# The feed-forward head of a two-layer encoder: the projection's last tiles and the norm's sums in a new order

## The chip, the cores and the metric

The kernel runs on one core of a Trainium2 chip. A core has a matrix engine (PE, with its weight loads shown apart as PEld), a vector engine (VectorE, DVE in the rows), a scalar engine (ScalarE, ACT), a general engine (GpSimd, POOL) and an engine that issues transfers (SyncE, SP). Each has its own queue and works it off in order; they meet at semaphores. The metric is the device time of the whole kernel in microseconds (us).

## The reference, cut to what matters

Two sequences, one of 256 and one of 512 tokens of width 1024, run through two layers and a last norm. Layer 0 mixes with an mLSTM, layer 1 with windowed attention; both then have the same feed-forward part.

```python
for l in range(DEPTH):                       # 2
    mod = silu(c) @ adaln_w[l] + adaln_b[l]  # sh1, sc1, g1, sh2, sc2, g2
    h = rmsnorm(x, norm_g[l, 0]) * (1 + sc1) + sh1
    y = mixer(h)                             # ends with a projection: ... @ w_out
    x = x + g1 * y
    h = rmsnorm(x, norm_g[l, 1]) * (1 + sc2) + sh2
    x = x + g2 * conv_ffn(h, w_up, conv_w, conv_b, w_down)
return rmsnorm(x, final_g)
```

All is float32. The change sits where the mixer's projection ends (`x = x + g1 * y`), the second norm follows (`rmsnorm(x, norm_g[l, 1])`), and the feed-forward's first products begin.

## The kernel before, in words

The 768 tokens stand side by side, columns of tiles with 128 features as rows; they are worked in two halves of 384. A float32 weight is split into a high part in the matmul's format (cast on ScalarE, `whi`, L260) and the low rest (difference on VectorE, `wlo`, L261); a product takes three matmuls: high by high, high by low, low by high.

**The projection** (`out_proj`, L592) is a generator. It makes 16 tiles of 128 features by 384 tokens: tiles 0 to 7 for the first half, 8 to 15 for the second. The weights come from another generator (`tiles`, L596): a tile's weights are loaded, cast and split only when the loop at L619 asks for them. Tiles 8 to 10 use weights that are still there; those of tiles 11 to 15 are loaded again. A tile is 24 matmuls into one of four fixed PSUM banks (tile i goes to bank (i + 2) mod 4), then the residual sum on VectorE (L590), then its square on ScalarE (L111). The generator stops ahead of tile 8 and of tile 15, in each case with that tile's weights already fetched. The weights' high parts and low parts have three buffers each, the raw loads five.

**The norm** (`Norm`, L90). The first six of a half's eight squares are summed on VectorE (L115) as they come; the other two stay apart. So the mean over features is taken on PE from three tiles: three tiles by three blocks of 128 tokens, each a matmul against a column of 1/1024; every one of them is two instructions in the trace, 18 in all. ScalarE adds epsilon (L150), GpSimd raises to the power -1/2 (L153), PE broadcasts the result over the rows (6 instructions), and `apply` (L1095) scales, shifts and, for the second half, forms the combinations of quarters that the feed-forward's products need (T1 to T4, by a scheme with seven products for eight). The first half's `apply` is issued whole; the second's is a generator whose steps the head calls one by one. Its first work on VectorE is the difference of two shifts, `dsh` (L1108), a tile of 128 x 4.

**The head** (`head`, L1257, called at L1412) begins the feed-forward while the projection ends. It stands in a block with a manual schedule for PE, ScalarE and VectorE (L1411): what the block issues on these three runs in the order in which it is written. Everything else is ordered by a planner that simulates the engines; instructions from outside the block may be put between those of the block. GpSimd and SyncE are the planner's throughout. The head as written before the change:

1. loads of the first two weight units (`ra`, `rb`, twice);
2. two "marks": small matmuls that open banks 2 and 3 (L1276, L1436);
3. split of `ra[0]` (`wa[0]`); the weight sums `sums(0)` (L1279: four differences and sums of 512 columns, one more for the low part of the sum, one cast); split of the result (`wc[0]`);
4. the rest of the projection, that is tile 15 with residual sum and square (L1300);
5. the product B11 by `wa[0]` (12 matmuls), the copy of its bank to `r1` (L1189), the norm's mean, `sums(1)`, the split `wc[1]`, the product B21 into the same bank, the copies to `r1` (L1182), the norm's broadcast and its first combination (L1304 to L1311);
6. the other products, with the norm's steps between (from L1313).

**Behind the head** the pairs of feed-forward units follow (`pair`, L1194). A pair's weight sums run on GpSimd (L1202, L1205, L1206, L1214). For the first pairs, `issue_after` (L1420) queues their instructions on ScalarE and VectorE behind two instructions that the head returns; those on GpSimd are free. So the pair's first sums may run on GpSimd while the head works.

Of the kernel before, what the change touches and what calls it, by code (L numbers as in the profile page):

```python
# [11 lines left out]
F32 = mybir.dt.float32  # L12
# [72 lines left out]
def pieces(c0, c1):  # L85

    return [(max(c0, s0), min(c1, s1), q) for q, (s0, s1) in enumerate(SEQS) if max(c0, s0) < min(c1, s1)]


class Norm:  # L90
# [16 lines left out]
    def square(self, c):  # L107

        net = self.net
        sq = net.tmp([P, self.n])  # L110
        net.nc.scalar.activation(sq, self.x(c), AF.Square)  # L111
        self.sums.append(sq)
        if 2 <= len(self.sums) and self.count < KC - self.on_pe:
            acc = self.sums[0]
            self.adds.tensor_tensor(acc, acc, self.sums.pop(), ALU.add)  # L115
        self.count += 1
# [3 lines left out]
    def begin(self, n):  # L120

        if self.pm is None:
            self.pm = self.net.pa()
            self.sides = [self.pm[:, 2 * b : 2 * b + 2] for b in range(self.n // P)]
            self.done = 0
        for i in range(self.done, n):
            for b, o in enumerate(self.sides):

                self.net.nc.tensor.matmul(
                    o, self.sums[i][:, b * P : (b + 1) * P], self.net.inv,  # L130
                    start=i == b == 0, stop=i == KC - 1, skip_group_check=True,
                )
        self.done = max(self.done, n)

    def stages(self):
# [17 lines left out]
        nc.gpsimd.tensor_tensor(r, r, net.mhalf[:, :nb], ALU.pow)  # L153
# [14 lines left out]
class Net:  # L168
# [423 lines left out]
    def out_proj(self, u0, act, xt, l, apply):  # L592
# [16 lines left out]
        norms = [Norm(self, xt, half, apply, last=True, adds=self.nc.vector) for half in HALVES]  # L609
# [9 lines left out]
        for i, (z, c, w) in enumerate(todo):  # L619
            if i in (KC, 2 * KC - 1):  # L620
                yield
            c0, c1, _ = HALVES[z]
            o = self.ps()[:, : c1 - c0]
            self.product(o, w, act, c0, c1, range(self.begun.pop(i, 0), KC))
            self.tick(4.2)
            for p0, p1, q in pieces(c0, c1):
                self.resid(xt, o[:, p0 - c0 : p1 - c0], l, 16, c, (p0, p1, q))
            norms[z].square(c)
            if i % KC == KC - 1:
                self.start(HALVES[z], norms[z].stages())  # L630
# [443 lines left out]
    def combined(self, l, i, pool):  # L1074
# [19 lines left out]

        def apply(x, pr, rng):  # L1095
            if rng[0] == 0:
                for c in range(KC):
                    full[c] = one(F32)
                    modulate(full[c], c, x, pr, rng)
                    put((self.B11, self.B21)[c // 4], c % 4, full[c])  # L1100
                return
# [5 lines left out]
            dsh = pool.tile([P, 4], F32, name="dsh")  # L1107
            nc.vector.tensor_tensor(  # L1108
                dsh, self.mod[l][:, 24 * i + 4 : 24 * i + 8, q], self.mod[l][:, 24 * i : 24 * i + 4, q], ALU.subtract
            )  # L1110
# [73 lines left out]
    def outset(self, o, w, r1):  # L1184
# [3 lines left out]
        self.quarters(o, part(0), self.B11, True)  # L1188
        self.nc.scalar.copy(r1[:, col(H) :], o)  # L1189
        yield  # L1190
        self.quarters(o, part(1), self.B21, False)
# [65 lines left out]
    def head(self, u0, last_tile, pool, urows, mark, early):  # L1257
# [21 lines left out]
        def sums(i):  # L1279
# [4 lines left out]
            tt(s2, s1_, s2, ALU.subtract)  # L1284
            tt(s4, s4, s2, ALU.subtract)
            tt(s1[i][1], s1_, s1[i][0].bitcast(F32), ALU.subtract)
            tt(s1_, a22, s2, ALU.subtract)

# [9 lines left out]
        sums(0)  # L1298
        wc[0] = self.split(ra[0])
# [4 lines left out]
        first = self.outset(fixed(0), wa[0], rows[0][0])  # L1304
        next(first)
        step()
        sums(1)
        wc[1] = self.split(ra[1])
        next(first, None)

        step()  # L1311
# [57 lines left out]
        return act.ins, dve.ins  # L1369
# [298 lines left out]
```

## Time and profile before

| what | value |
|---|---|
| median of 3 runs | 1844.58 us (1842.21 to 1845.0) |
| profiled execution | 1843.78 us, its span 1842.0 |
| PE busy | 1793.2 us, 97% of the span |
| VectorE busy | 1367.0 us, 74% |
| ScalarE busy | 895.3 us, 49% |
| GpSimd busy | 488.0 us, 26% |
| mean granted clock of PE | 0.994 |
| the head of layer 0 | from about 500 us |
| the head of layer 1 | from about 1290 us |

How to read the rows. In the order of time a row has the start, the duration, the engine, the line of the kernel, the operation, output and input tiles, their shape and the count; in brackets stands how long the engine had been idle and what ended that. Matmuls are pipelined: a row's duration reaches over the start of the next, so that the distance of starts is the cost. In the view by windows a row has the stretch, its length, the busy time of PE, PEld, DVE, ACT and POOL with their counts, the granted clock of PE (1.00 is full speed), the share of the transfer engines and GB/s. The chain of waits is the work that ended last, followed back from the end.

### The profile page before, as it was taken

How to read it: one execution, taken by the hardware profiler on the slowest of the kernel's cores; microseconds unless marked ns; L12 is line 12 of the kernel's file. 1: busy time of each engine (PE TensorE's matmuls, PEld its weight loads, DVE VectorE, ACT ScalarE, POOL GpSimd, SP SyncE). 2: the span in 40 equal slices, each digit the busy share in tenths (PEclk: the TensorE clock that was granted, in tenths of full speed). 3: DMA queues.
4: the chain of work that ended last, by engine and by line, in shares of the span. 5: the costliest groups of instructions: out<-in, count | busy, mean ns of one | idle time of the engine just before them, and what ended most of it. 6: DMA issues, size and time to landing. Idle time of an engine off the chain costs nothing.

```text
span 1842.0 us, 28931 instructions
## 1 busy us (share of the span) xinstructions
PE 1793.2 (97%) x11290; PEld 1657.4 (90%) x11290; DVE 1367.0 (74%) x2101; ACT 895.3 (49%) x1815; POOL 488.0 (26%) x386
## 2 busy tenths in 40 slices
PE   6999999999999999999999999999999999999997
PEld 3987887889998999999999999889989999999997
DVE  4755676886689877777777757766898777777776
ACT  4443443354456444444444556765564444444443
POOL 1001001021024333333331313430144333333322
PEclk9999999999999999999999999999999999999999
DMA  8344566546312221222223321124122222222212
GB/s 330 119 145 134 172 195 221 164 138 219 101 46 74 76 61 66 69 69 69 69 69 93 104 83 50 53 94 129 50 86 69 69 69 69 69 69 70 69 35 69
DMA packets 64245, 184.48 MB, mean 100 GB/s; under 512 B 6167, under 2 KB 23831, under 8 KB 64108
## 3 DMA queue, kind: packets, MB, share of 16 engines
q1 hardware_dynamic: 64108, 182.63, 30.8%
q8 instruction: 89, 1.46, 0.3%
q14 instruction: 48, 0.39, 0.1%
HBM read 176.17 MB, written 6.43 MB: 99 GB/s over the span
## 4 chain that ended last, share of the span: by engine, by line
PE 86%; DVE 6%; DMA 3%; ACT 2%; issue 1%; POOL 1%; SPq 0%; POOLq 0%; ACTq 0%; DVEq 0%
PE ps L254 27%; PE pa L254 25%; PE ps L1169 10%; PE ps L1172 10%; PE ps L1170 10%; PE pa L1008 1%; DMA slab<-in_adaln_w_dram 1%; DMA raw<-in_w_dram 1%; DVE wlo L261 1%; DVE ada L506 1%; DVE slab L590 1%; DMA raw<-in_adaln_w_dram 0%; PE pa L1172 0%; PE pa L1169 0%; PE pa L1170 0%
## 5 line engine op out<-in xcount | busy, mean ns | idle before, releaser
L260 ACT CAST whi<-raw 128x1024 fp32r<-128x1024 f32 x237 | 247.9, 1048 | 350.4 <-PE pa L254 161.4
L261 DVE TENSOR_TENSOR wlo<-raw,whi 128x1024 fp32r<-128x1024 f32 x237 | 316.6, 1337 | 119.8 <-ACT whi L260 117.3
L254 PE MATMUL pa<-slab,whi 128*128 128x256 f32 (+1 forms) x1472 | 346.6, 331 | 3.2 <-DVE slab L590 3.2
L254 PEld LDWEIGHTS pa<-slab,whi 128*128 128x128 f32 x1472 | 252.7, 188 | 27.5 <-DVE slab L590 4.5
L590 DVE SCALAR_TENSOR_TENSOR slab<-pa,mod,slab 128x256 f32<-128x256 f32 (+1 forms) x368 | 211.2, 592 | 70.8 <-PE pa L254 70.5
L254 PE MATMUL pa<-slab,wlo 128*128 128x256 f32 (+1 forms) x736 | 233.9, 330 | 0.0
L254 PE MATMUL ps<-zh,whi 128*128 128x256 f32 (+1 forms) x560 | 189.0, 339 | 2.3 <-ACT whi L260 1.7
L254 PE MATMUL ps<-zh,wlo 128*128 128x256 f32 (+1 forms) x560 | 184.1, 330 | 2.0 <-DVE wlo L261 2.0
L254 PE MATMUL ps<-zl,whi 128*128 128x256 f32 (+1 forms) x560 | 185.1, 332 | 0.0
L1169 PE MATMUL ps<-zh,whi 128*128 128x384 f32 x504 | 172.3, 342 | 3.6 <-ACT nt L1240 1.8
L1170 PE MATMUL ps<-zl,whi 128*128 128x384 f32 x504 | 169.9, 337 | 0.8 <-DVE zl L1126 0.8
L1172 PE MATMUL ps<-zh,wlo 128*128 128x384 f32 x504 | 168.9, 335 | 0.0
L254 PEld LDWEIGHTS pa<-slab,wlo 128*128 128x128 f32 x736 | 138.5, 188 | 13.1 <-DVE wlo L261 0.4
L1205 POOL TENSOR_TENSOR raw<-raw,raw 128x512 f32<-128x512 f32 x40 | 52.2, 1305 | 330.8 <-DVE wlo L261 259.4
L254 PE MATMUL ps<-slab,whi 128*128 128x384 f32 x512 | 132.0, 339 | 0.9 <-DVE slab L261 0.5
L1402 POOL TENSOR_TENSOR slab<-slab 128x772 f32<-128x772 f32 x44 | 86.5, 1967 | 164.6 <-DVE slab L1390 152.7
L1389 DVE SCALAR_TENSOR_TENSOR slab<-slab,cstt,slab 128x771 f32<-128x771 f32 x88 | 103.6, 1179 | 26.6 <-ACT slab L1387 26.5
L254 PEld LDWEIGHTS ps<-zh,whi 128*128 128x128 f32 x560 | 107.4, 192 | 15.9 <-issue 4.4
L506 DVE SCALAR_TENSOR_TENSOR ada<-raw,silc,ada 128x1024 f32<-128x1024 f32 x84 | 110.6, 1354 | 14.9 <-DMA raw<-in_adaln_w_dram 14.8
L1202 POOL TENSOR_TENSOR raw<-raw 128x512 f32<-128x512 f32 x40 | 68.5, 1712 | 200.1 <-DMA raw<-in_w_dram 169.7
L254 PEld LDWEIGHTS ps<-zh,wlo 128*128 128x128 f32 x560 | 107.2, 192 | 12.2 <-DVE wlo L261 2.9
L254 PEld LDWEIGHTS ps<-zl,whi 128*128 128x128 f32 x560 | 107.4, 192 | 11.9 <-issue 3.4
(291 smaller groups left out, 4265.7 us busy)
## 6 DMA issues: line engine op xcount, KB each, us to landing
raw<-in_w_dram SPq DMA_DIRECT2D x208, 512.0 KB, 3.7
raw<-in_adaln_w_dram SPq DMA_DIRECT2D x84, 512.0 KB, 4.6
slab<-in_x_dram SPq DMA_DIRECT2D x12, 512.0 KB, 6.8
slab<-in_adaln_w_dram SPq DMA_DIRECT2D x12, 512.0 KB, 10.3
slab<-mrows SPq DMA_DIRECT2D x8, 384.0 KB, 5.3
xs<-slab SPq DMA_DIRECT2D x6, 512.0 KB, 3.6
bt<-brow SPq DMA_DIRECT2D x16, 192.0 KB, 3.0
slab<-xs SPq DMA_DIRECT2D x6, 512.0 KB, 6.9
```

The source lines that it names most:

```text
L254: self.nc.tensor.matmul(out, lhsT, rhs, start=start, stop=stop)
L260: nc.scalar.copy(hi, src)
L261: return nc.vector.tensor_tensor(lo, src, hi.bitcast(F32), ALU.subtract)
L506: stt(acc[:, s], row, w, acc[:, s], ALU.mult, ALU.add)
L590: self.nc.vector.scalar_tensor_tensor(x, o, self.mod[l][:, gc + c, q : q + 1], x, ALU.mult, ALU.add)
L1169: mm(o, wh[:, k], hi[k], start=start and k == 0, stop=False, skip_group_check=True)
L1170: mm(o, wh[:, k], lo[k], start=False, stop=False, skip_group_check=True)
L1172: mm(o, wl[:, k], hi[k], start=False, stop=k == 3, skip_group_check=True)
L1202: tt(q[2], q[2], q[3], ALU.add)
L1205: tt(q[0], q[2], q[0], ALU.subtract)
L1389: stt(y[:, 1:], u[:, :-1], w(0), y[:, 1:], ALU.mult, ALU.add)
L1402: nc.gpsimd.tensor_tensor(y, y, yrow[:, j], ALU.mult)
```

## The change

Five things.

- The projection's generator stops ahead of tile 14 instead of tile 15, and for tiles 14 and 15 also between product and residual sum and behind the square. The head resumes it step by step, with the weight sums `sums(0)` and `sums(1)`, now generators too, in between. So tile 14 comes into the block, behind the marks, and so does all that the generator issues when it is resumed.
- In this order the first weight sums come ahead of tile 14's residual sum, the second's first two ahead of tile 15's.
- The first half sums all eight squares on VectorE (`on_pe` 0), the second seven (`on_pe` 1): the mean has one and two tiles on PE instead of three. The second half's first tile goes to PE right behind tile 15 (`begin(1)`), the other after eight matmuls of B11.
- `outset` takes the norm's steps into the products: B11's first eight matmuls, the mean, its last four, the copy, B21's first eight, the broadcast, its last four.
- `dsh` is formed in the first half's `apply`. The head also returns the norm's power, so that the first pairs' instructions on GpSimd are queued behind it.

```diff
 class Norm:
     def square(self, c):
         ...
         self.sums.append(sq)
-        if 2 <= len(self.sums) and self.count < KC - self.on_pe:
+        self.count += 1
+        if not self.held:
+            self.add()
+
+    def add(self):
+        if 2 <= len(self.sums) and self.count <= KC - self.on_pe:
             acc = self.sums[0]
             self.adds.tensor_tensor(acc, acc, self.sums.pop(), ALU.add)
-        self.count += 1
+
+    held = False
...
-        for i in range(self.done, n):
+        last = min(KC, self.on_pe + 1) - 1
+        for i in range(self.done, min(n, last + 1)):
...
-        nc.gpsimd.tensor_tensor(r, r, net.mhalf[:, :nb], ALU.pow)
+        self.power = nc.gpsimd.tensor_tensor(r, r, net.mhalf[:, :nb], ALU.pow)

 def out_proj(...)
-        norms = [Norm(self, xt, half, apply, last=True, adds=self.nc.vector) for half in HALVES]
+        norms = [Norm(self, xt, half, apply, i, last=True, adds=self.nc.vector) for i, half in enumerate(HALVES)]
+        self.norm = norms[1]
...
         for i, (z, c, w) in enumerate(todo):
-            if i in (KC, 2 * KC - 1):
+            late = i >= 2 * KC - 2
+            if i in (KC, 2 * KC - 2):
                 yield
             ...
             self.tick(4.2)
+            if late:
+                norms[z].held = True
+                yield
             for p0, p1, q in pieces(c0, c1):
                 self.resid(xt, o[:, p0 - c0 : p1 - c0], l, 16, c, (p0, p1, q))
             norms[z].square(c)
+            if late:
+                yield

 def combined(...)
+        dsh = pool.tile([P, 4], F32, name="dsh")
+
         def apply(x, pr, rng):
             if rng[0] == 0:
+                s = self.mod[l][:, 24 * i : 24 * i + 8, 0]
+                nc.vector.tensor_tensor(dsh, s[:, 4:], s[:, :4], ALU.subtract)
...
-    def outset(self, o, w, r1):
+    def outset(self, o, w, r1, low=None):
-        self.quarters(o, part(0), self.B11, True)
+        self.quarters(o, part(0), self.B11, True, low)
         self.nc.scalar.copy(r1[:, col(H) :], o)
         yield
-        self.quarters(o, part(1), self.B21, False)
+        self.quarters(o, part(1), self.B21, False, low)

 def head(...)
         def sums(i):
             ...
             tt(s2, s1_, s2, ALU.subtract)
+            yield
             tt(s4, s4, s2, ALU.subtract)
+            yield
             tt(s1[i][1], s1_, s1[i][0].bitcast(F32), ALU.subtract)
             tt(s1_, a22, s2, ALU.subtract)
+            yield
...
         wa[0] = self.split(ra[0])
-        sums(0)
-        wc[0] = self.split(ra[0])
+        ops = [sums(i) for i in range(2)]
+        next(ops[0])
+        next(ops[0])
+        wc[0], low = split(ra[0])
+        next(last_tile)
+        next(last_tile)
+        next(ops[0])
+        low()
+        self.norm.add()
+        next(last_tile)
+        self.norm.begin(1)
+        next(ops[1])
+        next(last_tile)
+        next(ops[1])
+        wc[1], low = split(ra[1])
+        next(ops[1])
+        low()
         for _ in last_tile:
             pass
         norm = self.take(HALVES[1])
         step = lambda n=1: [next(norm, None) for _ in range(n)]
-        first = self.outset(fixed(0), wa[0], rows[0][0])
+        first = self.outset(fixed(0), wa[0], rows[0][0], step)
         next(first)
-        step()
-        sums(1)
-        wc[1] = self.split(ra[1])
         next(first, None)
-        step()
...
-        return act.ins, dve.ins
+        return act.ins, dve.ins, self.norm.power.ins
```

More of the change, by code (lines that the diff above doesn't have):

```diff
@@ L130, in begin @@
                     o, self.sums[i][:, b * P : (b + 1) * P], self.net.inv,
-                    start=i == b == 0, stop=i == KC - 1, skip_group_check=True,
+                    start=i == b == 0, stop=i == last, skip_group_check=True,
                 )
@@ L1106, in apply @@
             sh = lambda c: self.mod[l][:, 24 * i + c, q : q + 1]
[L1107 to L1110, printed above, removed]
             def scale(c):
```

## The prediction

> **What bounds the kernel now.** I read the page's busy times and its chain first, then the waits of the matmul engine, then the order of time around the feed-forward head of layer 0 (500 to 520 us) on each engine, then layer 1 for the same places, and last the granted clock wherever PE had been idle. The page, its busy line and its chain:
>
> ```profile
> span 1842.0 us, 28931 instructions
> PE 1793.2 (97%) x11290; PEld 1657.4 (90%) x11290; DVE 1367.0 (74%) x2101; ACT 895.3 (49%) x1815; POOL 488.0 (26%) x386
> PE 86%; DVE 6%; DMA 3%; ACT 2%; issue 1%; POOL 1%; SPq 0%; POOLq 0%; ACTq 0%; DVEq 0%
> ```
>
> PE sets the end, so the change is worth the matmuls it takes out and the gaps it closes or opens on PE in two places, one per layer. A stretch of layer 0, from the view by windows (its length, then PE's busy time): PE has no gap in the six tiles ahead of the head.
>
> ```profile
> 477.60:501.40 23.80, 23.80 (x147) 23.80 (x146) 18.87 (x37) 16.29 (x36) 0.85 (x1) 1.00 0.29 90
> ```
>
> PE alone in order of time (start, duration, x count): marks, tile 15, B11, the 18 small matmuls of the mean, B21, the broadcast of the norm, and the next product.
>
> ```profile
> 505.57 0.52 PE L254 MATMUL ps<-yh 128*128 128x384 f32 x2
> 505.93 0.52 PE L254 MATMUL ps<-slab,whi 128*128 128x384 f32 x2
> ...
> 510.12 0.34 PE L1169 MATMUL ps<-yh,whi 128*128 128x384 f32 x1
> ...
> 512.21 2.06 PE L254 MATMUL pa<-inv,nt 128*128 128x2 f32 x18
> 514.13 0.42 PE L1169 MATMUL ps<-yh,whi 128*128 128x384 f32 x1
> ...
> 516.12 0.34 PE L1172 MATMUL ps<-yh,wlo 128*128 128x384 f32 x1
> 516.93 0.93 PE L254 MATMUL pa<-kct,nr 128*128 128x128 f32 x6 [0.47 <-POOL nr L153]
> ```
>
> A tile's 24 matmuls take 510.12 - 505.93 = 4.19 us, 0.175 each; the 18 of the mean take 514.13 - 512.21 = 1.92, 0.107 each. The broadcast could have gone at 516.30 and went at 516.93.
>
> VectorE, ScalarE and GpSimd there:
>
> ```profile
> 498.20 1.04 ACT L260 CAST whi<-raw 128x1024 fp32r<-128x1024 f32 x1
> 501.56 0.62 DVE L590 SCALAR_TENSOR_TENSOR slab<-ps,mod,slab 128x384 f32<-128x384 f32 x1
> 502.10 0.55 DVE L115 TENSOR_TENSOR nt<-nt,nt 128x384 f32<-128x384 f32 x1
> 505.77 0.62 DVE L590 SCALAR_TENSOR_TENSOR slab<-ps,mod,slab 128x384 f32<-128x384 f32 x1 [0.93 <-PE ps L254]
> 508.06 0.69 DVE L1286 TENSOR_TENSOR s1l<-raw,s1h 128x512 fp32r<-128x512 f32 x1
> 508.78 0.69 DVE L1287 TENSOR_TENSOR raw<-raw,raw 128x512 f32<-128x512 f32 x1
> 509.39 1.22 DVE L261 TENSOR_TENSOR wlo<-raw,whi 128x1024 fp32r<-128x1024 f32 x1
> 511.17 0.53 ACT L111 ACTIVATE nt<-slab 128x384 f32<-128x384 f32 x1 [1.86 <-DVE slab L590]
> 512.40 0.48 ACT L1189 COPY slab<-ps 128x384 f32<-128x384 f32 x1 [0.71 <-PE ps L1172]
> 514.30 1.30 POOL L1205 TENSOR_TENSOR raw<-raw,raw 128x512 f32<-128x512 f32 x1 [5.94 <-DMA raw<-in_w_dram]
> 515.02 1.13 DVE L1286 TENSOR_TENSOR slab<-raw,slab 128x512 fp32r<-128x512 f32 x1 [1.84 <-ACT slab L1283]
> 515.57 1.31 POOL L153 TENSOR_TENSOR nr<-nr,mhalf 128x3 f32<-128x3 f32 x1
> 517.93 1.25 DVE L1108 TENSOR_TENSOR dsh<-mod 128x4 f32<-128x4 f32 x1
> ```
>
> What to see: the cast at 498.20 begins the weights of tile 15, more than six microseconds before PE's tile at 505.93; its difference follows on VectorE ahead of the row at 501.56. At 515.02 VectorE idled 1.84 us for one operand though L1287, behind it in the written order, had all it needed: the block's order binds. The power (L153) stood behind the pair's L1205 on GpSimd, hence PE's gap before the broadcast.
>
> **The change, step by step** (per layer; layer 0's numbers).
>
> *First half's mean.* All eight squares are summed on VectorE, so 18 small matmuls become 6: 12 x 0.107 = **-1.28**. The two added VectorE sums (0.55 as at 502.10) fall where that engine waits for tiles; PE has no gap after, so the gain is kept.
>
> *Second half's mean.* 18 become 12, six of them ahead of B11: **-0.64**. The last six wait for tile 15's square: by the times below it is ready 0.6 us before them, so nothing is added.
>
> *The power.* issue_after puts the pair's GpSimd sums behind it: it no longer waits for L1205, and PE's gap goes: 516.93 - 516.30 = **-0.63** (in layer 1 the row below has 0.76 idle where layer 0 has 0.47: -0.92). The pair's sums start some 5 us later; their readers come after the head's last products, 25 us on, so they cost nothing; without that cover the price would be their own 1.3 us each. No transfer waits for the power; SyncE's loads keep their order but for one, next.
>
> ```profile
> 1307.70 0.93 PE L254 MATMUL pa<-kct,nr 128*128 128x128 f32 x6 [0.76 <-POOL nr L153]
> ```
>
> *The split of tile 15's weights moves.* This decides the case. The generator of the projection fetches a tile's weights when its loop comes to that tile. Before, it stopped at i = 15 with those weights fetched, outside the block. Now it stops at i = 14; the fetch of tile 15 (load, cast, difference) is issued when it is resumed the third time, inside the block, behind norm.add(). So on ScalarE the cast stands behind tile 14's square, on VectorE the difference stands behind tile 14's residual, s1l, s1_, the difference of wc[0] and the added sum. None of these can start before tile 14 ends on PE, and PE's next work in the written order is tile 15. Call T the slot after tile 14's last matmul. Residual at T + 0.20 (505.77 - 505.57); then, 0.54 to what follows it (502.10 - 501.56), 0.72 from s1l to s1_ (508.78 - 508.06), 0.61 to the difference of wc[0] (509.39 - 508.78), 1.22 for that, 0.55 for the sum and 1.22 for tile 15's difference, less some 0.15 by which neighbours overlap: ready at T + 4.9. Tile 15's first two matmuls need only the cast (residual 0.62, square 0.53, cast 1.04: T + 2.4); the third needs the difference, and would have gone at T + 0.35. Bubble 4.55, and 0.1 for the slower first matmul (514.13 to 514.39 instead of 0.175): **+4.65**. Its load moves behind the four loads of the head; it takes the raw buffer freed by tile 14's own difference, 8 us ahead of use, so the transfer is hidden. The bounds: 0 if the cast were pulled ahead, 6.5 if the residual also waits for a weight sum and the mark.
>
> *The marks move.* Two matmuls that open banks 2 and 3 stood behind tile 14; now they stand ahead of it, right behind tile 13, whose result lies in bank 3. The second mark waits for tile 13's residual: PE's slot would be 501.56, the residual ends at 501.56 + 0.62 = 502.18. With the restart **+0.8** (0 if the residual were done, 1.5 if a weight sum of 0.7 goes first).
>
> *B21 right behind the copy.* outset now runs through in one go: the copy of the bank (L1189) had the 18 small matmuls to hide under; now B21 writes the same bank next. From the slot after B11, 512.21, to the copy's end at 512.88 is 0.67; with hand-over and restart, 0.18: **+0.85**. The bounds are 0 and 1.9, the cast of wc[1] in front of it on ScalarE. The broadcast's six matmuls follow eight of B21, so the power is in time.
>
> *Shift difference.* 1.25 us leave VectorE's path to the first scaling (it ended with the pair's L1206 on GpSimd); in the first half it costs some tenths beside tile 11. Together with the missing 1.84 wait VectorE starts the combinations some 2 us earlier against PE. I count that as nothing: what follows on it is paced by copies that ScalarE takes from PE in the written order (last part). It could be worth up to the gaps of rival 2.
>
> *The clock.* After PE had idled 2.18 us in front of another product, this is what the trace shows (PE in order of time, then stretches of the view by windows, whose number after the engines is the granted clock):
>
> ```profile
> 1060.17 0.43 PE L254 MATMUL pa<-zl,whi 128*128 128x256 f32 x1 [2.18 <-DVE zl L552]
> 1061.04 0.41 PE L254 MATMUL pa<-zh,wlo 128*128 128x256 f32 x1
> 1061.25 0.41 PE L254 MATMUL pa<-zh,whi 128*128 128x256 f32 x1
> ...
> 1064.16 0.28 PE L254 MATMUL pa<-zh,whi 128*128 128x256 f32 x1
> 1064.28 0.28 PE L254 MATMUL pa<-zl,whi 128*128 128x256 f32 x1
> 20.00:25.00 5.00, 2.59 (x20) 0.41 (x12) 4.42 (x7) 2.63 (x8) 3.17 (x5) 1.00 1.04 416
> 1060.00:1064.00 4.00, 3.83 (x19) 3.84 (x20) 3.90 (x10) 2.39 (x8) 0.00 (x0) 0.57 0.24 64
> ```
>
> Matmuls come every 0.21 instead of 0.12 us; a mean of 0.57 over four microseconds, with half as the low value, is 3.4 us at half clock, which loses 3.4 x (1 - 0.12/0.21) = 1.5 us. The new bubble idles PE for 2.2 and again 2.0 us with two matmuls between. The other row, 20 to 25 us, shows a similar idle time with the clock at 1.00. The bubble is nearer to the first (idle in front of dense matmuls, and twice); since part of the slow stretch may fall into the idle time, I take **+1.3**, between 0 and 2 x 1.5.
>
> The sum: -1.28 - 0.64 - 0.63 + 4.65 + 0.8 + 0.85 + 1.3 = +5.05 in layer 0, +4.76 in layer 1, +9.8 together. The profiled execution took 1843.78 (span 1842.0), which gives 1853.6; the median of the runs is 0.8 above it: **1854.4**.
>
> **The rivals.**
> 1. *The clock stays up in the bubble.* The row of 20 to 25 us speaks for it, that of 1060 against. 9.8 - 2.6 = +7.2: 1851.8. The Trainium skill, "TensorE: Matmul & The Clock Gate", section "What's actually happening", has the clock fall after at least one idle window of about 3.4 us; the bubble's two idle pieces are each shorter, so by that sentence this rival would hold. The trace at 1060 does not agree: 2.18 us were enough.
> 2. *The delay is hidden further on.* From 549 to 574 us VectorE is busy all the time and PE, third in the row, is not: gaps of 25.00 - 22.03 = 3.0 us a layer, which a late PE could find closed: 9.8 - 6.0 = +3.8, 1848.4. Against it: VectorE's work there hangs, by the chain of waits, on a copy that ScalarE takes from PE, and would come as late as PE.
>
> ```profile
> 549.00:574.00 25.00, 22.03 (x121) 21.04 (x122) 24.96 (x24) 19.28 (x31) 12.93 (x7) 1.00 0.34 106
> 532.54 0.19 ACT slab L1182
> ...
> 533.53 0.56 DVE zl L1126
> ```
>
> 3. *Faster: the order does not bind what the resumed generator issues.* Then tile 15's weights are cast when a buffer is free, as at 498.20, and tile 14 runs ahead of the marks; bubble, slow clock and mark vanish, the copy stays: -1.70 and -1.99, 1840.9, and under that if VectorE's head start shortens any later wait. It decides as soon as the bubble is under 1.7 us. The row at 515.02 speaks against it.
>
> 4. *Worse*: two slow stretches a layer, a weight sum ahead of each residual: +13, 1858.
>
> **How the numbers follow.** Forecast 0.58, rival 1 0.20, rival 2 0.07, rival 3 0.05, rival 4 0.10. The range 1848 to 1859 leaves out rival 3, the lower edge of 2 and what lies beyond 4; the forecast's own range is 1852 to 1857. The chances: faster 0.04, same 0.06, slower 0.90. Slower by over 0.2% (3.7 us, about what a measurement tells from no change) holds the forecast, 1, 4 and part of 2; faster is rival 3.
>
> **What would show it.** Right: PE idle right after tile 14, first for the cast, then for tile 15's difference (L261); a clock near half for some 3 us behind it; a mark that waits for L590; L1170 or L1169 waiting for L1189; 6 and 12 mean matmuls; no wait for L153. Wrong: tile 15's difference ahead of tile 14's residual on VectorE, or gaps of 539 to 573 shrunk by as much as the bubble.

## The result, and the profile after

The changed kernel took **1855.07 us** (median of 6 runs, 1854.66 to 1857.34) against 1844.79 us for the kernel before beside it: ratio **1.0059, 95% interval 1.0049 to 1.0070**, slower by some 10 us of 1845. The profiled execution of the changed kernel, on which all rows of it below are taken, was the longest of its six: 1857.34 us, span 1855.6. Against the profiled execution of before that is 13.6 us, and it is these 13.6 us that the rows have to account for, not the 10.

The page of the changed kernel, its span, the busy line and the shares of the chain:

```profile
span 1855.6 us, 28863 instructions
PE 1794.1 (97%) x11254; PEld 1655.8 (89%) x11254; DVE 1376.3 (74%) x2107; ACT 895.0 (48%) x1815; POOL 485.7 (26%) x386
PE 84%; DVE 7%; ACT 4%; DMA 3%; issue 1%; POOL 1%; SPq 0%; POOLq 0%; ACTq 0%; DVEq 0%
```

36 recorded matmuls fewer (11290 before), yet PE is busy 0.9 us longer: some of its matmuls became slower. And PE's share of the chain went from 86 to 84%, to VectorE and ScalarE, for which it now waits.

PE alone in order of time, head of layer 0 (start, duration; the line numbers of the changed kernel are 7 to 14 above those of before: L254 is now L261, L260 is L267, L590 is L597, L1169 is L1183, L1189 is L1203). The first two rows are the marks, the third is the last of tile 14, the next two are tile 15, then the two parts of the mean (B11's first eight products lie between them), B21, the broadcast and the next product:

```profile
500.30 0.34 PE L261 MATMUL ps<-yh 128*128 128x384 f32 x1
502.15 0.44 PE L261 MATMUL ps<-yh 128*128 128x384 f32 x1 [1.51 <-DVE slab L597]
506.45 0.34 PE L261 MATMUL ps<-slab,wlo 128*128 128x384 f32 x1
508.99 0.62 PE L261 MATMUL ps<-slab,whi 128*128 128x384 f32 x2 [2.20 <-ACT whi L267]
511.56 0.69 PE L261 MATMUL ps<-slab,wlo 128*128 128x384 f32 x1 [1.96 <-DVE wlo L268]
518.24 0.72 PE L136 MATMUL pa<-inv,nt 128*128 128x2 f32 x6
520.30 0.72 PE L136 MATMUL pa<-inv,nt 128*128 128x2 f32 x6
522.40 0.44 PE L1183 MATMUL ps<-yh,whi 128*128 128x384 f32 x1 [0.57 <-ACT slab L1203]
523.89 0.83 PE L261 MATMUL pa<-kct,nr 128*128 128x128 f32 x6
525.25 0.34 PE L1183 MATMUL pa<-yh,zh 128*128 128x384 f32 x1
```

Four waits that before did not have: one for a residual sum (the mark), two for the weights of tile 15, one for the copy of the bank. None before the broadcast at 523.89, where before waited 0.47 for the power. VectorE and ScalarE at the same place show why tile 15 waits:

```profile
500.88 0.68 DVE L1296 TENSOR_TENSOR raw<-raw 128x512 f32<-128x512 f32 x1
501.48 0.61 DVE L597 SCALAR_TENSOR_TENSOR slab<-ps,mod,slab 128x384 f32<-128x384 f32 x1
...
506.82 0.62 DVE L597 SCALAR_TENSOR_TENSOR slab<-ps,mod,slab 128x384 f32<-128x384 f32 x1 [2.60 <-PE ps L261]
507.90 1.03 ACT L267 CAST whi<-raw 128x1024 fp32r<-128x1024 f32 x1
508.68 1.22 DVE L1310 TENSOR_TENSOR wlo<-raw,whi 128x1024 fp32r<-128x1024 f32 x1
509.82 0.55 DVE L120 TENSOR_TENSOR nt<-nt,nt 128x384 f32<-128x384 f32 x1
510.29 1.22 DVE L268 TENSOR_TENSOR wlo<-raw,whi 128x1024 fp32r<-128x1024 f32 x1
```

The cast of tile 15's weights, at 498.20 before, runs at 507.90, behind tile 14's residual sum (506.82); its difference (L268, 510.29) is the fifth operation that VectorE does behind that sum. At 500.88 a weight sum stands ahead of tile 13's residual sum, for which the mark at 502.15 waits.

The view by windows (the number after the engines' busy times is the granted clock): the head of layer 0 from 510 us on, the same place in layer 1, and the 26 us some 31 us behind the head. The bubble is PE's idle time between tiles 14 and 15.

```profile
510.00:518.00 8.00, 6.44 (x21) 6.44 (x22) 2.80 (x4) 0.62 (x1) 0.22 (x2) 0.57 0.45 131
1306.00:1313.00 7.00, 5.17 (x17) 4.72 (x17) 3.55 (x5) 0.00 (x0) 0.22 (x2) 0.51 0.46 152
556.63:582.63 26.00, 22.95 (x127) 21.86 (x128) 25.96 (x24) 20.15 (x33) 13.47 (x7) 1.00 0.34 102
```

And for comparison the row of the kernel **before** for the 26 us that begin as far (31.38 us) behind the same product:

```profile
549.00:575.00 26.00, 23.03 (x126) 22.00 (x127) 25.96 (x24) 20.17 (x33) 13.68 (x7) 1.00 0.33 102
```

With half speed as the low value (the single microseconds from 512 to 517 show 0.50), a mean of 0.57 over 8 us is 6.9 us of slow clock, a mean of 0.51 over 7 us is the same. Behind the head the delay stays: PE's gaps in the two stretches are 2.97 and 3.05 us, and the product ahead of them that waits for a low part of weights shows what is left of the delay there (before, then the changed kernel):

```profile
548.96 0.98 PE L1176 MATMUL pa<-zh,wlo 128*128 128x384 f32 x4 [0.22 <-DVE wlo L1293]
556.45 0.96 PE L1190 MATMUL pa<-zh,wlo 128*128 128x384 f32 x4 [0.22 <-DVE wlo L1310]
```

It comes 7.49 us later, where the head's first product with zh came 7.63 later (525.25 against 517.62): all but 0.14 us of the delay is still there.

Where the time came from, layer 0, in starts on PE (a slot is when a matmul would have gone without a wait): the mark +1.7 (its slot was 500.30 + 0.175, it went at 502.15), the bubble +4.6 (tile 15's third matmul at 511.56; the slot after tile 14 is 506.45 + 0.17 = 506.62, and the third would have gone 0.35 later), the slow clock +2.75 (tile 15's last 22 matmuls took 518.24 - 511.56 = 6.68 us, at 0.175 each, and 0.08 more for the first behind a wait, they take 3.93), the copy +0.8, the matmuls taken out -1.28 - 0.64, the gap at the broadcast -0.63: **+7.3**. In starts of the two ends (from the ninth-last residual sum before the head's first product with zh to that product, 44.00 before) the head grew to 51.34: +7.3. Layer 1 grew from 44.13 to 50.65, +6.5.

### The profile page after: what moved, and what is told of

Its sections match the earlier page's. It is cut to its first block, busy times and chain, and to the rows that moved or that the text cites. A ratio compares the mean times of both kernels' runs of the same rounds, so it can differ in the third digit from the quotient of the medians.

```text
span 1855.6 us, 28863 instructions
## 1 busy us (share of the span) xinstructions
PE 1794.1 (97%) x11254; PEld 1655.8 (89%) x11254; DVE 1376.3 (74%) x2107; ACT 895.0 (48%) x1815; POOL 485.7 (26%) x386
## 4 chain that ended last, share of the span: by engine, by line
PE 84%; DVE 7%; ACT 4%; DMA 3%; issue 1%; POOL 1%; SPq 0%; POOLq 0%; ACTq 0%; DVEq 0%
PE ps L261 26%; PE pa L261 25%; PE ps L1183 10%; PE ps L1184 10%; PE ps L1186 10%; PE pa L1022 1%; DVE wlo L268 1%; DMA slab<-in_adaln_w_dram 1%; DVE slab L597 1%; ACT whi L267 1%; ACT bq L1107 1%; DMA raw<-in_w_dram 1%; DVE ada L513 1%; DMA raw<-in_adaln_w_dram 0%; PE pa L1186 0%
## 5 line engine op out<-in xcount | busy, mean ns | idle before, releaser
L267 ACT CAST whi<-raw 128x1024 fp32r<-128x1024 f32 x233 | 243.7, 1048 | 337.5 <-PE pa L261 160.4
L268 DVE TENSOR_TENSOR wlo<-raw,whi 128x1024 fp32r<-128x1024 f32 x233 | 318.1, 1366 | 115.6 <-ACT whi L267 113.2
L261 PE MATMUL pa<-slab,whi 128*128 128x256 f32 (+1 forms) x1472 | 346.6, 331 | 3.2 <-DVE slab L597 3.2
L261 PEld LDWEIGHTS pa<-slab,whi 128*128 128x128 f32 x1472 | 252.6, 188 | 27.7 <-DVE slab L597 4.9
L597 DVE SCALAR_TENSOR_TENSOR slab<-pa,mod,slab 128x256 f32<-128x256 f32 (+1 forms) x368 | 211.5, 593 | 68.1 <-PE pa L261 67.7
L261 PE MATMUL pa<-slab,wlo 128*128 128x256 f32 (+1 forms) x736 | 234.0, 330 | 0.0
L261 PE MATMUL ps<-zh,whi 128*128 128x256 f32 (+1 forms) x560 | 189.1, 339 | 2.7 <-ACT whi L267 2.1
L261 PE MATMUL ps<-zh,wlo 128*128 128x256 f32 (+1 forms) x560 | 184.0, 330 | 2.0 <-DVE wlo L268 2.0
L261 PE MATMUL ps<-zl,whi 128*128 128x256 f32 (+1 forms) x560 | 185.4, 333 | 0.0
L1183 PE MATMUL ps<-zh,whi 128*128 128x384 f32 x504 | 172.3, 342 | 3.8 <-ACT nt L1254 2.0
L1184 PE MATMUL ps<-zl,whi 128*128 128x384 f32 x504 | 169.9, 337 | 1.7 <-DVE zl L1140 1.7
L261 PEld LDWEIGHTS pa<-slab,wlo 128*128 128x128 f32 x736 | 138.5, 188 | 13.2 <-DVE wlo L268 0.4
L261 PE MATMUL ps<-slab,whi 128*128 128x384 f32 x512 | 136.1, 347 | 5.3 <-ACT whi L267 4.7
L1417 DVE SCALAR_TENSOR_TENSOR slab<-slab,cstt,slab 128x771 f32<-128x771 f32 x88 | 105.5, 1201 | 26.8 <-ACT slab L1415 26.6
L261 PEld LDWEIGHTS ps<-zh,whi 128*128 128x128 f32 x560 | 107.3, 192 | 16.3 <-issue 4.4
L261 PEld LDWEIGHTS ps<-zh,wlo 128*128 128x128 f32 x560 | 107.3, 192 | 12.2 <-DVE wlo L268 2.9
L261 PEld LDWEIGHTS ps<-zl,whi 128*128 128x128 f32 x560 | 107.5, 193 | 12.0 <-issue 3.4
L1418 DVE SCALAR_TENSOR_TENSOR slab<-slab,cstt,slab 128x771 f32<-128x771 f32 x88 | 110.9, 1260 | 0.8
```

The source lines that it names most:

```text
L261: self.nc.tensor.matmul(out, lhsT, rhs, start=start, stop=stop)
L267: nc.scalar.copy(hi, src)
L268: return nc.vector.tensor_tensor(lo, src, hi.bitcast(F32), ALU.subtract)
L597: self.nc.vector.scalar_tensor_tensor(x, o, self.mod[l][:, gc + c, q : q + 1], x, ALU.mult, ALU.add)
L1183: mm(o, wh[:, k], hi[k], start=start and k == 0, stop=False, skip_group_check=True)
L1184: mm(o, wh[:, k], lo[k], start=False, stop=False, skip_group_check=True)
```

## The experiments

Each was compared with the kernel before on the same chip. Their trace is read above all by the **length of the head**: from the start of the ninth-last residual sum on VectorE to the first product with zh on PE. It leaves out what other parts of the program do from run to run (in the eleven executions of the table that residual sum starts anywhere between 473.0 and 476.2 us in layer 0).

| kernel | ratio to before, 95% | head, layer 0, us | head, layer 1, us |
|---|---|---|---|
| before | 1 | 44.00 | 44.13 |
| changed | 1.0059 (1.0049 to 1.0070) | 51.34 | 50.65 |
| changed, tile 15 fetched ahead | 0.9976 (0.9967 to 0.9986) | 43.40 | 43.39 |
| changed, PE kept busy in the bubble | 1.0043 (1.0029 to 1.0057) | 48.66 | 48.56 |
| before, tile 15 fetched late | 1.0051 (1.0032 to 1.0070) | 46.43 | 48.94 |
| fetched ahead, marks back | 0.9974 (0.9965 to 0.9983) | 42.56 | 42.55 |
| the same, copy under the mean | 0.9977 (0.9968 to 0.9986) | 42.21 | 42.18 |
| before, sums on VectorE | 0.9986 (0.9978 to 0.9995) | 41.43 | 41.32 |
| before, pairs behind the power | 1.0015 (1.0005 to 1.0025) | 43.27 | 43.11 |
| before, both | 0.9998 (0.9989 to 1.0007) | 41.24 | 41.10 |
| before, both and shift difference | 0.9977 (0.9968 to 0.9986) | 41.24 | 41.11 |

### Is it the fetch of tile 15's weights? (the change with the fetch ahead)

The generator of the projection hands out tiles 14 and 15 only when the weights of both are fetched; all else is the changed kernel.

```diff
-            for u in range(2):
-                for h, w in self.halves(u0 + u):
-                    yield 1, 2 * u + h, w
+            for h, w in self.halves(u0):
+                yield 1, h, w
+            for h, w in list(self.halves(u0 + 1)):
+                yield 1, 2 + h, w
```

> The changed kernel, with one edit: the generator of the weights fetches the last two tiles' weights together, so that the split of tile 15's weights is issued ahead of the head's block; all else stays, the two tiles in the block too. Fetch theory (the bubble ahead of tile 15 and the slow clock behind it come from the split of its weights standing in the block): both waits of PE ahead of tile 15 (2.20 and 1.96 us in layer 0) go, the clock stays at 1.00, and 4.7 us of bubble plus 1.3 to 2.8 us of slow clock leave each layer: 12 to 15 us under the changed kernel, 1840 to 1844, about the kernel before or a little under it, with the mark's wait and the copy's wait left. Order rival (it is the written order of residual, weight sums and squares that holds PE, whoever issues the weights): PE still waits some 2 to 4 us between the tiles, and the time stays above 1849.

1841.09 us. PE's waits in the head of layer 0 are only these two (PE in order of time; L1184 is the changed kernel's L1183):

```profile
500.65 0.44 PE L261 MATMUL ps<-yh 128*128 128x384 f32 x1 [0.91 <-DVE slab L597]
513.55 0.44 PE L1184 MATMUL ps<-yh,whi 128*128 128x384 f32 x1 [0.57 <-ACT slab L1204]
```

Both waits of tile 15 are gone, the granted clock is 1.00 in both heads, and the head is 7.9 and 7.3 us shorter than the changed kernel's. One moved fetch turned a gain of 0.24% into a loss of 0.59%.

### Is the slow clock a cost of its own? (the change with PE kept busy)

26 matmuls into a bank that nobody reads fill the bubble; nothing else is changed.

```diff
         next(last_tile)
+        spin = self.pa()[:, :H]
+        for _ in range(26):
+            mark(spin)
         next(last_tile)
```

> The changed kernel, with 26 matmuls more in each layer that fill PE's bubble: right behind tile 14, into a bank that nobody reads (26 x 0.175 = 4.55 us, the bubble being 4.6). Nothing is made earlier. Clock theory (the idle bubble halves the granted clock behind it, a price of its own): the clock stays at 1.00 through tile 15, its 22 matmuls behind the wait take 3.9 us instead of 6.7, and the kernel gets faster by 1.5 to 2.8 us a layer though it does more: 1849.5 to 1852. Rival (the slow matmuls of tile 15 have another cause, such as their operands or the transfers beside them): tile 15 stays slow and the time stays at 1855 or above.

1852.38 us, with more work. PE in order of time, then the view by windows:

```profile
507.35 4.67 PE L261 MATMUL pa<-yh 128*128 128x384 f32 x26
511.86 0.51 PE L261 MATMUL ps<-slab,whi 128*128 128x384 f32 x2
512.29 0.44 PE L261 MATMUL ps<-slab,wlo 128*128 128x384 f32 x1
516.25 0.72 PE L136 MATMUL pa<-inv,nt 128*128 128x2 f32 x6
```

```profile
510.00:514.00 4.00, 4.00 (x24) 3.77 (x23) 3.52 (x5) 0.00 (x0) 0.11 (x1) 1.00 0.51 143
```

The third matmul of tile 15 comes at 512.29 - 507.35 = 4.94 us after the slot, exactly as in the changed kernel, and what follows takes 3.96 us instead of 6.68, at clock 1.00. So the bubble's own cost is the same and the clock's is the rest. In the traces the two heads are 2.68 and 2.09 us shorter than the changed kernel's. All four heads of the changed kernel that were traced have a slow stretch, and neither of these two has. The times alone do not show the gain: 1852.38 is 2.7 us less than 1855.07, but the intervals of the two ratios overlap (1.0029 to 1.0057 and 1.0049 to 1.0070).

### The fetch alone, in the kernel before

```diff
-            if i in (KC, 2 * KC - 1):
+            if i == KC:
                 yield
...
             norms[z].square(c)
+            if i == 2 * KC - 2:
+                yield
```

> The kernel before, with one part of the change alone: the generator stops behind tile 14 instead of ahead of tile 15 with the weights fetched, so the split of tile 15's weights is issued in the block, behind that of wc[0]; tile 14, marks, sums, power and shift difference as before. Fetch theory: the cast waits for tile 14's buffer (three for the high parts), so PE waits behind tile 14 for a cast and a difference, 1.05 + 1.2 us and hand-overs, 2.3 to 2.6 us a layer, and then perhaps a slow clock of 1.5 us: slower than before by 4.6 to 8 us, 1849.5 to 1853. Order rival: the weight sums and squares stand as before, so the time stays within 1 us of before.

1853.65 us. PE in order of time, both layers, and two windows:

```profile
508.28 0.62 PE L254 MATMUL ps<-slab,whi 128*128 128x384 f32 x2 [0.88 <-ACT whi L260]
510.63 0.44 PE L254 MATMUL ps<-slab,wlo 128*128 128x384 f32 x1 [1.73 <-DVE wlo L261]
...
1299.89 0.61 PE L254 MATMUL ps<-slab,whi 128*128 128x384 f32 x2 [1.00 <-ACT whi L260]
1302.12 0.69 PE L254 MATMUL ps<-slab,wlo 128*128 128x384 f32 x1 [1.61 <-DVE wlo L261]
```

```profile
1301.00:1308.00 7.00, 5.88 (x18) 5.88 (x19) 1.06 (x1) 0.00 (x0) 2.53 (x4) 0.52 0.45 150
508.00:516.00 8.00, 5.99 (x33) 5.67 (x34) 3.78 (x5) 1.18 (x3) 1.90 (x3) 1.00 0.42 131
```

The late fetch by itself makes a bubble (3.05 us here: the slot is 508.28 - 0.88 - 0.17, the third matmul comes 3.40 behind it instead of 0.35) and a loss of 0.51% without any other part of the change, both a little over what was expected (2.3 to 2.6 us, up to 1853 us). It also shows the clock: the same 2.6 us of idle time in two pieces brought 6.7 us of slow clock in layer 1 and none in layer 0, and the heads grew by 4.8 and 2.4. Whether a slow stretch comes is not set by the idle time alone.

### The changed kernel once more

> The changed kernel once more, for one look: is the slow stretch behind the bubble the same in another execution? Fetch and clock theory: the same bubble (2.2 and 2.0 us of idle in layer 0), a slow stretch in both layers, of one or two times 3.4 us according to where the bubble falls; a time of 1853 to 1858. If the clock had nothing to do with the bubble, the stretch would lie elsewhere.

1858.01 us in a single run. The waits were the same four in both layers (1.51, 2.20, 1.96, 0.57 in layer 0). Of the slow clock, layer 0 had one stretch this time and layer 1 two:

```profile
512.00:516.00 4.00, 3.47 (x12) 3.47 (x13) 1.77 (x3) 0.00 (x0) 0.15 (x2) 0.57 0.75 243
516.00:520.00 4.00, 4.00 (x28) 4.00 (x26) 1.93 (x4) 1.73 (x3) 0.08 (x1) 1.00 0.04 14
1307.00:1314.00 7.00, 5.06 (x16) 5.07 (x17) 3.18 (x5) 0.00 (x0) 0.22 (x2) 0.53 0.49 149
```

A mean of 0.57 over four is 3.4 us, 0.53 over seven 6.6. So the waits are fixed by the order, and the clock's cost differs between executions of one kernel: here one or two times some 3.4 us. The heads are 49.99 and 51.00 us long, together 1.0 us shorter than in the changed kernel's other trace; that this run was the longer one by 0.7 us comes from outside the heads.

### The marks, and the copy (on top of the fetch ahead)

First, the two marks behind tile 14 as before:

```diff
-        for t in banks[0][1:]:
-            mark(t)
...
         next(last_tile)
+        for t in banks[0][1:]:
+            mark(t)
         next(last_tile)
```

> The kernel of e1 (both weights fetched ahead) with the two marks issued behind tile 14 again instead of ahead of it. Mark theory (the second mark waits for tile 13's residual and holds tile 14): PE's wait of 0.91 and 1.01 us ahead of the second mark goes, with 0.1 us of restart: 2.1 us under e1, ratio to before near 0.9965. Rival (VectorE would only come to tile 14's or 15's operands that much later, so the wait moves): PE waits elsewhere in the head and the ratio stays at that of e1, 0.9976.

1840.14 us, a ratio of 0.9974 beside 0.9976 for the fetch alone: the intervals do not tell them apart. In the trace the mark's wait is gone and the heads are 0.84 and 0.84 us shorter, so the wait was real; of the 2.1 us expected the heads show 1.7.

Second, B11 in one piece and the norm's step behind the copy, so that the mean's matmuls cover it:

```diff
-        self.quarters(o, part(0), self.B11, True, low)
+        self.quarters(o, part(0), self.B11, True)
...
         next(first)
+        step()
         next(first, None)
```

> The kernel of e4 with B11 in one piece and the last six matmuls of the mean behind it, ahead of B21, as cover for the copy of the bank; B21 still has the broadcast ahead of its last four. Copy theory: PE's wait for the copy (0.57 us idle, 0.8 in slots) shrinks by the 0.64 us that the six matmuls take; the power is due some 0.7 us later, and eight matmuls of B21 (1.39 us) just cover it: 0.4 to 0.6 us a layer under e4, ratio to before near 0.996. Rival (the power becomes the wait): PE idles ahead of the broadcast instead and nothing is won.

1840.19 us, no gain in time, and the copy's wait went only from 0.57 to 0.46 and 0.40 us of idle time. The expectation missed: the copy now stands on ScalarE behind the cast of wc[1] (1.05 us), so the cover went to that. The heads are 0.35 and 0.37 us shorter.

### The other parts of the change, alone, in the kernel before

The squares summed on VectorE (all eight in the first half, seven in the second), nothing else:

```diff
-        norms = [Norm(self, xt, half, apply, last=True, adds=self.nc.vector) for half in HALVES]
+        norms = [Norm(self, xt, half, apply, i, last=True, adds=self.nc.vector) for i, half in enumerate(HALVES)]
```

> The kernel before with one part of the change alone: the squares summed on VectorE, eight in the first half and seven in the second; the mean of the second half stays in one piece behind B11. By the count of matmuls: 18 to 6 and 18 to 12, 0.107 us each, 1.92 us a layer, 3.8 us in all, ratio near 0.998, if nothing waits for the added sum. The gap ahead of the broadcast grows or stays, since the mean ends earlier and the power still stands behind the pair's sum: up to 0.6 us a layer of that is given back. Rival (VectorE has no room in the head, the added sum delays tile 15's residual): no gain, ratio 1.000.

1842.67 us. The heads are 2.6 and 2.8 us shorter, the whole gain of the three predicted steps (1.28 + 0.64 + 0.63, in layer 1 0.92 for the last), even without the power's step: the power ran at 513.93, ahead of the pair's sum. Behind the head's first product with zh a new wait takes part of it back: PE in order of time,

```profile
521.35 0.44 PE L1170 MATMUL pa<-yh,zh 128*128 128x384 f32 x1 [0.68 <-ACT slab L1190]
```

The pairs' sums behind the power, nothing else:

```diff
...
-        return act.ins, dve.ins
+        return act.ins, dve.ins, self.norm.power.ins
```

> The kernel before with one part alone: the pairs' sums on GpSimd are queued behind the norm's power. Power theory: PE's gap ahead of the broadcast (0.47 and 0.76 us idle) goes, 0.63 and 0.92 in slots, 1.5 us in all, ratio near 0.9992. Rival (the power is late by its own chain, mean, ScalarE, GpSimd): the gap stays. Second rival (the pairs' sums, now later, hold ScalarE's or VectorE's splits behind the head): the gap goes, but a wait for GpSimd appears after the head and the ratio is 1.000 or above.

1846.92 us: **slower**, although the gap before the broadcast is gone and the heads are 0.7 and 1.0 us shorter. VectorE, GpSimd, ScalarE and PE in order of time:

```profile
515.70 1.66 DVE L1288 TENSOR_TENSOR raw<-raw,raw 128x512 f32<-128x512 f32 x1
517.28 2.31 DVE L261 TENSOR_TENSOR wlo<-raw,whi 128x1024 fp32r<-128x1024 f32 x1
519.51 1.25 DVE L1109 TENSOR_TENSOR dsh<-mod 128x4 f32<-128x4 f32 x1
520.68 0.60 DVE L1114 SCALAR_TENSOR_TENSOR slab<-slab,gain,pa 128x384 f32<-128x384 f32 x1
515.33 1.48 POOL L1203 TENSOR_TENSOR raw<-raw 128x512 f32<-128x512 f32 x1
516.89 1.62 POOL L1206 TENSOR_TENSOR raw<-raw,raw 128x512 f32<-128x512 f32 x1
518.59 2.15 POOL L1207 TENSOR_TENSOR raw<-raw 128x512 f32<-128x512 f32 x1
522.39 0.47 ACT L1190 COPY slab<-pa 128x384 f32<-128x384 f32 x1
522.92 0.44 PE L1170 MATMUL pa<-yh,zh 128*128 128x384 f32 x1 [1.67 <-ACT slab L1190]
```

The three pair sums, kept back, now run in a row behind the power, just beside the end of the second weight sums. There VectorE's L1288 takes 1.66 us (the same operation of the first weight sums, L1287 in the prediction's rows, 0.69), the difference of wc[1] 2.31 (1.22), the shift difference 1.25. They end 0.55, 1.08 and 0.02 us after the GpSimd operations beside them (515.33 + 1.48 = 516.81, 518.51, 520.74). For the first two that is about what they take with GpSimd idle, from start to start (0.61 and 1.13 us in the kernel before, from 508.78 to 509.39 and from there to 510.52), as if each had begun its work only when GpSimd's operation was over. So the first scaling starts at 520.68, the cast and behind it in ScalarE's order the bank's copy come as late, and PE waits 1.67 for that copy. This is nearest to the second rival on record, though what PE waits for is ScalarE's copy and not GpSimd.

Both parts together, and then with the shift difference formed in the first half as well:

```diff
+        dsh = pool.tile([P, 4], F32, name="dsh")
+
         def apply(x, pr, rng):
             if rng[0] == 0:
+                s = self.mod[l][:, 24 * i : 24 * i + 8, 0]
+                nc.vector.tensor_tensor(dsh, s[:, 4:], s[:, :4], ALU.subtract)
...
```

> The kernel before with two parts of the change: the squares summed on VectorE and the pairs' sums on GpSimd queued behind the power. Theory (bunching): the power ends near 515.3 as with either part alone, the pairs' GpSimd sums then follow it without a gap from 515.3 on, VectorE's operations beside them stretch as in the run with the power's part alone (1.66 instead of 0.69, 2.31 instead of 1.22), and the first scaling, the cast behind it and the bank's copy on ScalarE come at the same late time, near 522.4, while PE is 1.28 us earlier still: one wait of 1.7 to 2.9 us a layer ahead of L1170's product with zh, and a time of 1844 to 1847, above that of the sums alone (0.9986). Rival: with the sums on VectorE the bunching no longer meets that path; the wait is 0.7 or less and the time 1841 to 1843, that of the sums alone or below it.

> The same with the shift difference moved into the first half as well: all of the change but the written order of the projection's last two tiles and of the weight sums. Theory: the shift difference (0.15 us alone, 1.25 us beside GpSimd) stood between the stretched operations and the first scaling; without it that scaling, the cast and the copy come some 1.2 us earlier, so the wait ahead of L1170's product shrinks by about 1.2 us against the run without this move, 2 x 1.2 = 2.4 us in time. Rival: the first scaling waits for something else (the power's product, the broadcast), the wait keeps its size within 0.3 us and the time is that of the other run.

1844.28 and 1841.27 us. PE in order of time in the first of these kernels, then VectorE, GpSimd and PE in the second:

```profile
520.86 0.44 PE L1170 MATMUL pa<-yh,zh 128*128 128x384 f32 x1 [1.67 <-ACT slab L1190]
```

```profile
517.57 0.60 DVE L1114 SCALAR_TENSOR_TENSOR slab<-slab,gain,pa 128x384 f32<-128x384 f32 x1
518.21 1.00 DVE L1131 SCALAR_TENSOR_TENSOR bq<-slab,mod,bq 128x384 f32<-128x384 f32 x1
516.64 2.16 POOL L1207 TENSOR_TENSOR raw<-raw 128x512 f32<-128x512 f32 x1
520.19 0.44 PE L1170 MATMUL pa<-yh,zh 128*128 128x384 f32 x1 [0.89 <-ACT slab L1190]
```

The wait of 1.67 us is the one of the power alone: the power's step gives back on VectorE's path what the sums had won, and 1844.28 is no better than the kernel before. Moving the shift difference takes 0.78 us of it away (1.2 were expected), and the time falls by 3.0 us, more than the 1.6 us of the two layers' waits explain. The rest of the 1.2 went to L1131, which now stands beside GpSimd's L1207 and takes 1.00 us instead of 0.62 (the 0.62 in the run with the power alone, at 521.32 behind GpSimd's row).

The Trainium skill, "SBUF — State Buffer", section "Who interferes with whom", says that a VectorE instruction with two inputs in SBUF contends with a GpSimd instruction that reads SBUF. These rows agree: L1131 with two large inputs of its own (slab, bq) stretches, while the scaling at 517.57, wholly beside the same L1207 but with one of its inputs the broadcast in pa, which PE writes, keeps its 0.60.

In the changed kernel the power's step brings PE no such wait. VectorE and GpSimd in order of time:

```profile
520.90 1.22 DVE L1310 TENSOR_TENSOR wlo<-raw,whi 128x1024 fp32r<-128x1024 f32 x1
522.81 1.29 POOL L1216 TENSOR_TENSOR raw<-raw 128x512 f32<-128x512 f32 x1
```

The second weight sums begin ahead of tile 15's residual sum there, so that the difference of wc[1] ends at 522.12, before the first pair sum starts. The pair's sums stretch VectorE's operations further on instead (L1144 takes 1.01 us at 526.59, L1140 1.65 at 527.52), but in layer 0 PE has no wait from the head's first product with zh up to 547.16.

So all of the change *but* the written order gives 0.9977, and all of it with the fetch ahead gives 0.9976. Beyond those parts, the written order is worth nothing that these runs can tell; it cost what its late fetch cost. The lowest median is that of the fetch ahead with the marks back, 1840.14 us, but its ratio, 0.9974, is not told apart from these two.

## Why the prediction was right

The forecast, 1854.4 us, and the sign came out; the sum stands on the steps as follows.

- **The split of tile 15's weights moves (+4.65).** Right in place, order and size: third matmul at T + 4.94 (T + 4.9 predicted), the first two at T + 2.4. It decided the case, as the prediction said: with the fetch ahead the loss is gone, and alone it makes a loss of 0.5%.
- **First and second half's mean (-1.28, -0.64) and the power (-0.63, -0.92).** Right in PE's order of time: six, six and six small matmuls, no wait for the last six, none before the broadcast. That the power's step costs nothing elsewhere was wrong in general. "The pair's sums start some 5 us later; their readers come after the head's last products, 25 us on, so they cost nothing" looked only at who reads the sums, not at who runs beside them. Alone, the step makes the kernel slower by 0.15%. In the changed kernel PE did not pay this price, because VectorE is through with the weight sums before the pair's sums start; that the steps depend on each other the prediction had not seen.
- **The marks move (+0.8).** Mechanism right, size wrong: 1.7. What failed is that nothing was counted ahead of tile 13's residual sum: the weight sum of 0.68 at 500.88 stood there. The prediction had this case as its upper bound, at 1.5.
- **B21 right behind the copy (+0.85).** Right: 0.57 us idle and 0.8 in starts, in both layers.
- **The clock (+1.3).** The mechanism was right, and rival 1 (the clock stays up) fell: half clock in both layers of both traces of the changed kernel, and with PE kept busy the clock stayed at 1.00 and tile 15 took 3.96 instead of 6.68 us. The size is not one number: in the profiled execution it was 2.75 us in layer 0, for two stretches of some 3.4 us, where the prediction had counted one; in the later execution layer 0 had one.
- **Shift difference (0).** Not separable in the changed kernel; beside the power's step, moving it won 0.78 us of a wait.
- **Rival 2** (the delay is hidden further on) fell: 7.49 of the head's 7.63 us of delay are still there at 556.45, and the gaps behind it are the same. VectorE's work there came as late as PE, as the prediction argued. **Rival 3** (the resumed generator's fetch is free to move) fell: the cast came behind tile 14's residual sum. **Rival 4** (two slow stretches a layer, a weight sum ahead of each residual sum, 1858) is close to what the profiled execution of 1857.34 was: two stretches in each layer, and a weight sum ahead of tile 13's residual sum. The later run of 1858.01 had three stretches, not four; the median of the runs lies under both.

So the total was nearer than its parts: in the profiled execution the marks and the clock cost 2 x (0.9 + 1.45) = 4.7 us more at most than predicted, of which layer 1 and the stretch between the layers gave back about one; the median lies 2.3 us under that execution. That the forecast came within 0.7 us of the median is thus luck in part: in the one execution whose steps were summed, the two heads grew by 13.9 us where 9.8 were predicted. Why the slow stretches fall differently in different executions was not settled.

## What to carry to other kernels

Where a generator is resumed inside a block whose order is kept, ask what it issues *before* it comes to the work you want there: here, it was the fetch of the next tile's weights, and a cast and a difference behind a residual sum cost 4.6 us a layer on the critical engine, where the move itself was worth nothing that the runs could tell. Price an idle time of PE in front of dense matmuls with the clock it may take along. And before calling work on another engine free, look also at what runs beside it at its new time, not only at who reads its result.

## What the runs showed of the hardware that was not expected

- The slow clock comes in units of some 3.4 us, none, one or two, for the same idle time: after 0.88 and 1.73 us of idle time none in layer 0, after 1.00 and 1.61 two in layer 1 of the same execution; after 2.20 and 1.96 two in one execution and one in the next. The Trainium skill, "TensorE: Matmul & The Clock Gate", section "What's actually happening", describes a window of about 3.4 us that runs freely and so meets the work at a different place each time. The unit and the difference between executions agree with that; that the clock falls only after a whole idle window, as the same section has it, does not: in each of these cases two matmuls lay between the idle pieces, and no piece was over 2.2 us.
- Beside a row of GpSimd sums, VectorE's operations on two inputs from SBUF, the on-chip memory of the tiles, took 1.66 instead of 0.69 us, 2.31 instead of 1.22, and a difference of 4 columns 1.25 instead of 0.15 (the 0.15 is from the kernel with the sums alone, at 519.04, where GpSimd's row had ended at 518.04).
